# An encoder block in fp32: GELU as one activation, a norm root moved behind the down products, and two more pairs of blocks by seven products

## Chip, cores and metric

The kernel runs on one core of a Trainium2 chip. The metric is the device time of one execution in microseconds. Engines are called by their names in the profile: PE is TensorE (PEld its weight loads), DVE is VectorE, ACT is ScalarE, POOL is GpSimd, SP is SyncE, which here only issues DMAs.

## What is computed

One layer of a bidirectional encoder on 256 tokens and 2048 features, all in fp32. Two attention branches are gated, merged and projected into the residual `x`; then comes the part that matters here, a gated MLP with 5632 hidden features (`D_FF`), and after it a gated embedding term and a last norm.

```python
def rms_norm(x, g):
    y = xf * lax.rsqrt(jnp.mean(xf * xf, axis=-1, keepdims=True) + RMS_EPS)
    return y * g
...
hf = rms_norm(x, ffn_norm[i])
g = dwconv_centred(hf @ w_ffn_gate[i], conv_w[i], conv_b[i])
x = x + (jax.nn.gelu(g) * (hf @ w_ffn_up[i])) @ w_ffn_down[i]
gate_p = jax.nn.sigmoid(rms_norm(x, ple_norm[i]) @ w_ple_gate[i])
x = x + gate_p * (p[i] @ w_ple_proj[i])
return rms_norm(x, final_norm)
```

`jax.nn.gelu` is the form with a tanh by default. The factor `rsqrt(...)` of a norm belongs to a token; it is called the root below.

## The kernel before

**Numbers in two parts.** PE multiplies in a type (`fp32r`) that keeps fewer bits, so each fp32 operand is split in a high and a low part: ScalarE copies it to the high part (L261 for weights, tile `whi`), VectorE subtracts that from the operand for the low part (L262, `wlo`). A product of two operands is three matmuls: high by high, high by low, low by high. Weights come in pieces of sixteen blocks of 128 x 128, by DMAs that SP issues (L238, tiles `raw`), and are split in parts of eight blocks (four at a pair's start). Four buffers each hold `whi` and `wlo`, so splitting runs at most a few parts ahead of PE.

**Jobs.** `_plan` writes the program out as a list of jobs, one after the other on PE. From L102 on:

- `gg`, `g` and `u`: one column block of the gate or up product each, 16 blocks of weights. `product` (L330) issues for each block one matmul with 512 columns (L324) and one with 256 (L325). The hidden features are done in two halves of 22 column blocks; in each half gate and up jobs alternate.
- `d0` and `d1`: the down product of each half, as two jobs (n = 0, 1) of 1024 output columns each.
- `pp` (embedding) and `pg` (its gate): four jobs each; then the output.

When a gate job is done, `after` (L766 to L778) adds its two partial results, multiplies by the root as a row over the tokens (`rt[1]`, L768), applies the convolution's three taps (L770 to L772) and computes the GELU from a square (L774, ScalarE), a product (L775, VectorE), a tanh (L776, ScalarE) and a last product (L777, VectorE). For an up job (L779 to L792) it multiplies by 0.5 and the root (L781) and by the GELU (L789), and splits the result for the down product into `act`; for the first 16 column blocks of a half it also builds sums of two neighbours (`add_up`, L797).

**Seven products in place of eight.** A down job goes over eleven pairs of hidden column blocks. A pair with 2 x 2 quarters (two token halves, two halves of 512 columns) can be done plainly, by eight products, or by seven products of sums of quarters; each product is three matmuls of 512 columns (L400 to L402), so 24 or 21 in all. `_pairs` (L126) gives the order of a job's pairs and which of them go by seven: for the last job, `d1` with n = 1, `[5, 0, 1, 6, 2, 3, 7, 4, 8, 9, 10]` and pairs 0 to 4; for the other three `[8, 0, 1, 2, 3, 9, 4, 5, 6, 7, 10]` and pairs 0 to 7. A pair by seven needs sums of quarters of its weights. They are built long before: POOL's queue fetches the quarters (L286, L287), VectorE subtracts (L299), POOL's queue writes the result to device memory (L303), and SP fetches it back when its pair comes near (L315). `sums_ahead` (in the loop over the jobs) hands this out over the jobs. One more sum is subtracted on the spot (L270), or fetched ready made for pairs 2, 3, 6 and 7 (`WHOLE`); another always on the spot (L272). So a pair by seven costs VectorE and ScalarE four splits (512, 1024, 1024, 1024 columns) and VectorE one or two subtractions of 512 columns.

**Ending a down job.** Four of the seven accumulators (p1, p5, p6, p7) are complete once the last pair by seven is done; then `spread_sums` (L827) runs: a copy of p1 on ScalarE (L830), four sums on VectorE (L835, L840, L841). At the end of the job the other four (p2, p3, p4, c22) follow (from L1085). Where the job is not the last of its columns, each result is written to a row buffer (tile `row`, seven of them, L819) and added to the residual by a DMA on POOL's queue (`to_residual`, L825); the four late ones are copied by ScalarE (L1090). In the last job (`end`) VectorE adds them to the residual in place (L845, and `joined`, L905), but for p1 and the sum with p7, which go by DMA.

**Order around the change.** `at((i, k), f)` puts work ahead of step k of job i; a pair counts two steps. In the last job, step 10 has the squares of the first 1024 columns (`squares_of`, L856, ScalarE), step 18 splits the embedding (`layered`), steps 17, 17, 19, 19 the transposes of features (`flip`: PE L866, ScalarE L454, VectorE L455) for the norm and the products of `pg`. The transposes use the two `pt` banks of PE's accumulator memory, in which p6 and p7 lie in this job. The other features follow in the `pp` jobs. Work marked `keep` holds its order on its engine; other instructions may be put in another order within an engine.

## Time and profile before

| what | us |
|---|---|
| median of 3 runs | 1468.25 |
| lowest and highest run | 1464.38, 1468.91 |
| span of the profiled execution | 1463.2 |
| PE busy | 1449.4 |
| DVE busy | 1137.2 |
| ACT busy | 832.9 |

The profiled execution has no time of its own beside its span, which goes from the first to the last instruction; the runs lie 1.2 to 5.7 us above it. The mean clock that was granted to PE is 0.998. In the profile a row of instructions has: start, duration (both us), engine, line, operation, output and inputs, shape, how often, and in brackets the idle time before it with what ended it. A row of groups has: line, engine, operation, tiles, shape, count, then busy time in us, mean ns of one, and idle time before them in us. A row of the table of windows has the window, its length and for each engine the busy time and the number of instructions.

### The profile page before, as it was taken

The page shows a single profiled execution, that of the slowest core. Times are in us where ns is not written, and L with a number is a line of the kernel's source. Part 1 is how long each engine was busy: PE and PEld are TensorE (multiplying, and loading weights), DVE is VectorE, ACT ScalarE, POOL GpSimd, SP SyncE. Part 2 cuts the span into 40 slices and gives each one's busy share as a digit, 9 for nine tenths or more (in the row PEclk, how much of TensorE's full clock was granted, in tenths as well). Part 3 has the DMA queues.
Part 4 walks back from the last instruction along what each step waited for, and adds up shares of the span by engine and source line. Part 5 has one row for each costly group of instructions (what it writes and reads, how often), then busy time and mean ns, then how long its engine had stood idle before and what let it go on. Part 6 is the DMA issues. An engine that isn't in the chain of part 4 may idle for free.

```text
span 1463.2 us, 20802 instructions
## 1 busy us (share of the span) xinstructions
PE 1449.4 (99%) x7507; PEld 1234.3 (84%) x7507; DVE 1137.2 (78%) x1653; ACT 832.9 (57%) x1196; POOL 107.3 (7%) x178
## 2 busy tenths in 40 slices
PE   9999999999999999999999999999999999999997
PEld 8888888888888888888888888888888888788886
DVE  7687665665665668889998989897999987988665
ACT  7465444444444456665566655675656555666654
POOL 0000000001111100201111100102110100010000
PEclk9999999999999999999999999999999999999999
DMA  9754555557888967978788786989878864797652
GB/s 322 245 177 159 172 170 171 188 178 262 286 314 294 354 229 254 296 237 283 269 293 270 273 284 212 285 287 304 279 273 282 289 244 159 266 294 249 217 193 89
DMA packets 111731, 362.17 MB, mean 248 GB/s; under 512 B 12804, under 2 KB 17924, under 8 KB 111500
## 3 DMA queue, kind: packets, MB, share of 16 engines
q1 hardware_dynamic: 88908, 292.80, 57.5%
q0 software_dynamic: 20560, 63.71, 14.4%
q10 hardware_dynamic: 2160, 4.33, 0.9%
q8 instruction: 59, 0.97, 0.3%
q14 instruction: 44, 0.36, 0.1%
HBM read 324.06 MB, written 27.30 MB: 240 GB/s over the span
## 4 chain that ended last, share of the span: by engine, by line
PE 96%; DVE 1%; issue 1%; DMA 1%; ACT 0%; POOL 0%; POOLq 0%; DVEq 0%; ACTq 0%
PE acc L324 28%; PE acc L325 14%; PE acc L356 9%; PE acc L358 9%; PE acc L357 9%; PE acc L401 7%; PE acc L400 7%; PE acc L402 7%; PE first L324 2%; PE first L325 1%; PE pt L669 1%; DMA raw<-in_wts 0%; PE pt L866 0%; DVE wlo L262 0%; PE sp L628 0%
## 5 line engine op out<-in xcount | busy, mean ns | idle before, releaser
L262 DVE TENSOR_TENSOR wlo<-raw,whi 128x1024 fp32r<-128x1024 f32 (+2 forms) x556 | 650.7, 1181 | 264.3 <-ACT whi L261 258.9
L261 ACT ACTIVATE whi<-raw 128x1024 fp32r<-128x1024 f32 (+2 forms) x556 | 564.2, 1025 | 473.5 <-PE acc L358 188.7
L324 PE MATMUL acc<-mov,whi 128*128 128x512 f32 x1840 | 642.2, 395 | 0.3 <-DVE mov L455 0.3
L325 PE MATMUL acc<-mov,wlo 128*128 128x256 f32 x1840 | 511.0, 278 | 0.0
L324 PEld LDWEIGHTS acc<-mov,whi 128*128 128x128 f32 x1840 | 345.0, 188 | 79.5 <-DVE mov L455 0.6
L325 PEld LDWEIGHTS acc<-mov,wlo 128*128 128x128 f32 x1840 | 346.0, 188 | 0.5
L356 PE MATMUL acc<-whi,mov 128*128 128x512 f32 (+1 forms) x512 | 196.5, 384 | 0.0
L358 PE MATMUL acc<-whi,mov 128*128 128x512 f32 (+1 forms) x512 | 196.3, 383 | 0.0
L357 PE MATMUL acc<-wlo,mov 128*128 128x512 f32 (+1 forms) x512 | 196.2, 383 | 0.0
L356 PEld LDWEIGHTS acc<-whi,mov 128*128 128x128 f32 x512 | 96.7, 189 | 19.3 <-DVE first L444 0.8
L358 PEld LDWEIGHTS acc<-whi,mov 128*128 128x128 f32 x512 | 96.6, 189 | 18.8
L357 PEld LDWEIGHTS acc<-wlo,mov 128*128 128x128 f32 x512 | 96.6, 189 | 18.4
L400 PE MATMUL acc<-whi,act 128*128 128x512 f32 x207 | 80.9, 392 | 0.2 <-ACT whi L261 0.2
L401 PE MATMUL acc<-wlo,act 128*128 128x512 f32 x207 | 80.9, 391 | 0.0
L402 PE MATMUL acc<-whi,act 128*128 128x512 f32 x207 | 80.6, 389 | 0.0
L825 POOL DMA_DIRECT2D x<-row x36 | 31.1, 879 | 380.0 <-ACT row L830 258.1
L262 DVE TENSOR_TENSOR wlo<-sums,whi 128x1024 fp32r<-128x1024 f32 x37 | 45.1, 1219 | 9.9 <-ACT whi L261 9.9
L400 PEld LDWEIGHTS acc<-whi,act 128*128 128x128 f32 x207 | 38.8, 188 | 9.5 <-ACT whi L261 1.5
L401 PEld LDWEIGHTS acc<-wlo,act 128*128 128x128 f32 x207 | 38.9, 188 | 8.9 <-DVE wlo L262 0.9
L401 PE MATMUL acc<-wlo,shl 128*128 128x512 f32 x116 | 45.6, 393 | 0.0
L402 PEld LDWEIGHTS acc<-whi,act 128*128 128x128 f32 x207 | 38.9, 188 | 8.0
L402 PE MATMUL acc<-whi,shl 128*128 128x512 f32 x116 | 45.2, 390 | 0.0
(203 smaller groups left out, 1669.5 us busy)
## 6 DMA issues: line engine op xcount, KB each, us to landing
raw<-in_wts SPq DMA_DIRECT2D x477, 512.0 KB, 5.0
sums<-kept SPq DMA_DIRECT2D x37, 512.0 KB, 5.6
sums<-in_wts POOLq DMA_DIRECT2D x23, 512.0 KB, 6.8
kept<-sums POOLq DMA_DIRECT2D x23, 512.0 KB, 4.1
raw<-in_wts SPq DMA_DIRECT2D x39, 256.0 KB, 4.9
row<-in_wts POOLq DMA_DIRECT2D x37, 256.0 KB, 8.2
x<-row POOLq DMA_DIRECT2D x36, 256.0 KB, 7.7
two<-in_wts POOLq DMA_DIRECT2D x14, 512.0 KB, 8.0
```

Of the source, the lines that this page charges most:

```text
L261: nc.scalar.activation(hi, src, AF.Copy)
L262: ins = nc.vector.tensor_tensor(lo, src, hi.bitcast(F32), op=ALU.subtract)
L324: nc.tensor.matmul(acc, hi[:, o, :], m, start=first, stop=False, skip_group_check=True)
L325: nc.tensor.matmul(acc[:, T:], lo[:, o, :], m[:, :T], start=False, stop=last, skip_group_check=True)
L356: nc.tensor.matmul(acc, xh, hi, start=(k == 0), stop=False)
L357: nc.tensor.matmul(acc, xh, lo, start=False, stop=False)
L358: nc.tensor.matmul(acc, xl, hi, start=False, stop=(k == n - 1))
L400: nc.tensor.matmul(acc, xh, hi, start=(e == 1), stop=False)
L401: nc.tensor.matmul(acc, xh, lo, start=False, stop=False)
L402: nc.tensor.matmul(acc, xl, hi, start=False, stop=(e == uses[name]))
L669: nc.tensor.transpose(p[:, k, t * P:(t + 1) * P], s[:, t, (c + k) * P:(c + k + 1) * P], ident)
L825: keep(nc.gpsimd.dma_start(quarter(n, t, c), a, accum_op=ALU.add))
```

## The change

The GELU becomes one activation with the tanh form. The up products are no longer multiplied by 0.5 and the root; since the root belongs to a token, it is applied to the down products' results instead, each time they are copied, scaled or added: as a scale from memory (`token_scale`) on ScalarE, or in a VectorE instruction that multiplies and adds. For this the first copy of p1 is made twice (unscaled for the sums, scaled for the residual), and finished sums that leave by DMA are scaled in place by ScalarE. The row of the first p1 copy then takes the last sum. In the last job, seven pairs go by seven products instead of five, in another order, and the transposes stand two steps later. The job list and everything ahead of the MLP stay the same.

```diff
-        return [5, 0, 1, 6, 2, 3, 7, 4, 8, 9, 10], range(5)
+        return [7, 0, 1, 2, 8, 3, 4, 5, 6, 9, 10], range(7)
...
-            w = ff.tile([P, T], F32, name="gw", bufs=2)
-            nc.scalar.activation(w, c, AF.Square, scale=math.sqrt(0.044715))
-            nc.vector.scalar_tensor_tensor(w, w, 1.0, c, op0=ALU.add, op1=ALU.mult)
-            nc.scalar.activation(w, w, AF.Tanh, scale=GELU_C)
-            nc.vector.scalar_tensor_tensor(c, w, 1.0, c, op0=ALU.add, op1=ALU.mult)
+            nc.scalar.activation(c, c, AF.Gelu_apprx_tanh)
             held["gelu", n] = c
         elif kind == "u":
             u = gather(acc)
-            nc.vector.scalar_tensor_tensor(u, u, 0.5, rt[1], op0=ALU.mult, op1=ALU.mult)
...
-    def spread_sums(n, bank, end):
-
+    def spread_sums(n, bank, end, scaled):
+
+        def add(t, c, a):
+            if end and c:
+                q = quarter(n, t, 1)
+                if scaled:
+                    nc.vector.scalar_tensor_tensor(q, a, token_scale(t), q, op0=ALU.mult, op1=ALU.add)
+                else:
+                    nc.vector.tensor_tensor(q, q, a, op=ALU.add)
+                return
+            if scaled:
+                nc.scalar.activation(a, a, AF.Copy, scale=token_scale(t))
+            to_residual(n, t, c, a)
+
+        base = row()
+        nc.scalar.activation(base, bank["p1"], AF.Copy)
+        if scaled:
+            first = row()
+            nc.scalar.activation(first, bank["p1"], AF.Copy, scale=token_scale(0))
+            to_residual(n, 0, 0, first)
+        else:
+            add(0, 0, base)
         u = row()
-        nc.scalar.activation(u, bank["p1"], AF.Copy)
-        to_residual(n, 0, 0, u)
...
+        nc.vector.tensor_tensor(u, bank["p6"], base, op=ALU.add)
+        v = row()
+        nc.vector.tensor_tensor(v, bank["p7"], u, op=ALU.add)
+        w = base if scaled else row()
+        nc.vector.tensor_tensor(w, bank["p5"], v, op=ALU.add)
         nc.vector.tensor_tensor(u, bank["p5"], u, op=ALU.add)
...
+        add(1, 0, v)
+        add(0, 1, u)
+        add(1, 1, w)
+
+    def token_scale(t):
+        return held["scale"][:, t:t + 1]
...
-    def joined(n, t, acc, parts):
+    def joined(n, t, acc, parts, scaled):
 
         r = res[:, t, n * W4:(n + 1) * W4]
-        nc.vector.tensor_tensor(r, acc, r, op=ALU.add)
+        if scaled:
+            nc.vector.scalar_tensor_tensor(r, acc, token_scale(t), r, op0=ALU.mult, op1=ALU.add)
+        else:
+            nc.vector.tensor_tensor(r, acc, r, op=ALU.add)
...
+            at((i + 3, 6), lambda: nc.vector.tensor_scalar(held["scale"], rc[1], 1.0, None, op0=ALU.mult))
...
-                                  [(i + 1, k) for k in (17, 17, 19, 19)]):
+                                  [(i + 1, k) for k in (19, 19, 21, 21)]):
...
-                    nc.scalar.activation(a, acc[name], AF.Copy)
+                    nc.scalar.activation(a, acc[name], AF.Copy, scale=1.0 if kind == "o" else token_scale(t))
```

More of the change, by code (lines that the diff above doesn't have):

```diff
@@ L44 @@
 TWINS = [slice(t, T, 2) for t in range(2)]
-GELU_C = math.sqrt(2.0 / math.pi)
 QA, KA, VA = 0, 8, 10
@@ L825, in to_residual @@
         keep(nc.gpsimd.dma_start(quarter(n, t, c), a, accum_op=ALU.add))
-    def spread_sums(n, bank, end):
-        u = row()
-        nc.scalar.activation(u, bank["p1"], AF.Copy)
-        to_residual(n, 0, 0, u)
-        last = u
-        for name in ("p6", "p7"):
-            v = row()
-            nc.vector.tensor_tensor(v, bank[name], last, op=ALU.add)
-            last, u = v, last
-        u, v = u, last
-        to_residual(n, 1, 0, v)
-        w = row()
-        nc.vector.tensor_tensor(u, bank["p5"], u, op=ALU.add)
-        nc.vector.tensor_tensor(w, bank["p5"], v, op=ALU.add)
-        for t, a in enumerate((u, w)):
-            if end:
-                q = quarter(n, t, 1)
-                nc.vector.tensor_tensor(q, q, a, op=ALU.add)
-            else:
-                to_residual(n, t, 1, a)
+    def spread_sums(n, bank, end, scaled):
[18 more added lines that the diff above has]
+            add(0, 0, base)
+        u = row()
+        nc.vector.tensor_tensor(u, bank["p6"], base, op=ALU.add)
[3 more added lines that the diff above has]
+        nc.vector.tensor_tensor(w, bank["p5"], v, op=ALU.add)
+        nc.vector.tensor_tensor(u, bank["p5"], u, op=ALU.add)
+        add(1, 0, v)
[3 more added lines that the diff above has]
+        return held["scale"][:, t:t + 1]
     def layered(pr):
@@ L971, in _encoder @@
                 held[a] = marks[:, e]
-            held["half"] = marks[:, 3, 0, :2]
+            held["half"], held["scale"] = marks[:, 3, 0, :2], marks[:, 4, 0, :2]
             for e in range(3):
@@ L1086, in _encoder @@
                 if end:
-                    joined(2 * n + c, t, acc[name], parts)
+                    joined(2 * n + c, t, acc[name], parts, kind != "o")
                 else:
                     a = row()
-                    nc.scalar.activation(a, acc[name], AF.Copy)
+                    nc.scalar.activation(a, acc[name], AF.Copy, scale=1.0 if kind == "o" else token_scale(t))
                     to_residual(n, t, c, a)
```

2 lines of the change are left out of this document (1 added, 1 removed).

## The prediction

> **What bounds the kernel now.** I read the page first, then the table of windows, then the time line of TensorE, then the other engines where a down job ends.
>
> ```profile
> span 1463.2 us, 20802 instructions
> PE 1449.4 (99%) x7507; PEld 1234.3 (84%) x7507; DVE 1137.2 (78%) x1653; ACT 832.9 (57%) x1196; POOL 107.3 (7%) x178
> PE 96%; DVE 1%; issue 1%; DMA 1%; ACT 0%; POOL 0%; POOLq 0%; DVEq 0%; ACTq 0%
> ```
>
> The third line is the chain that ended last: 96% of it is PE. A busy PE need not be PE at its pace, so the pace itself is read from starts. First a stretch of a gate or up job, then one of a down job (first and last row of each):
>
> ```profile
> 1195.08 0.40 PE L324 MATMUL acc<-mov,whi 128*128 128x512 f32 x1
> ...
> 1204.45 0.39 PE L324 MATMUL acc<-mov,whi 128*128 128x512 f32 x1
> ```
>
> ```profile
> 1332.11 0.39 PE L400 MATMUL acc<-whi,shl 128*128 128x512 f32 x1
> ...
> 1337.55 0.39 PE L400 MATMUL acc<-whi,act 128*128 128x512 f32 x1
> ```
>
> In the first, 27 blocks (a 512-column and a 256-column matmul each) take 9.37 us: 0.347 us each, 0.452 ns a column. In the second, 24 matmuls of 512 columns take 5.44 us: 0.2267 us each, 0.443 ns a column. The reader is to see that both stages issue at nearly the same time per column, though VectorE's load differs. What can be won is matmuls left out, and the few places where the pace breaks. The starts of the down stages, and of what follows them, give the size of these breaks:
>
> ```profile
> 884.32 0.39 PE L400 MATMUL acc<-whi,act 128*128 128x512 f32 x1
> ...
> 994.08 0.39 PE L324 MATMUL acc<-mov,whi 128*128 128x512 f32 x1
> ...
> 1239.46 0.40 PE L400 MATMUL acc<-whi,act 128*128 128x512 f32 x1
> ...
> 1338.24 1.03 PE L866 MATMUL pt<-ident,x 128*128 128x128 f32 x8
> ...
> 1353.67 0.39 PE L356 MATMUL acc<-whi,pw 128*128 128x512 f32 x1
> ```
>
> A pair by seven products is 21 matmuls, one by eight is 24. Both jobs of d0 and the first of d1 have 8 x 21 + 3 x 24 = 240, the last 5 x 21 + 6 x 24 = 249. So d0 should last 480 x 0.2267 = 108.8 us and lasts 109.8: 1.0 lost. d1 should last 489 x 0.2267 = 110.9, with two sets of eight transposes (0.8 each) 112.4, and lasts 114.2: 1.8 lost. Together 2.8 us.
>
> **The change, part by part.** *GELU and the norm root.* These groups go (one activation takes their place):
>
> ```profile
> L781 DVE SCALAR_TENSOR_TENSOR u<-u,rms 128x256 f32<-128x256 f32 x44 | 18.6, 424 | 1.1
> L775 DVE SCALAR_TENSOR_TENSOR gw<-gw,c 128x256 f32<-128x256 f32 x44 | 18.5, 421 | 2.7 <-ACT gw L774 2.7
> L777 DVE SCALAR_TENSOR_TENSOR c<-gw,c 128x256 f32<-128x256 f32 x44 | 18.4, 419 | 2.6 <-ACT gw L776 2.6
> L776 ACT ACTIVATE gw<-gw 128x256 f32<-128x256 f32 x44 | 18.3, 416 | 30.0 <-DVE gw L775 30.0
> L774 ACT ACTIVATE gw<-c 128x256 f32<-128x256 f32 x44 | 18.1, 411 | 8.6 <-DVE c L772 8.1
> ```
>
> VectorE loses 44 x (424 + 421 + 419) ns = 55.6 us. ScalarE loses 827 ns and gains one GELU each time; no row shows it; between nothing and the 827 ns of both I take the 416 of the Tanh, the nearest row: 18.1 us saved. Of this, what reaches the end?
>
> ```profile
> 660.00:890.00 230.00, 230.00 (x1321) 200.87 (x1320) 205.58 (x363) 135.66 (x215) 23.82 (x44) 1.00 0.78 269
> 1294.20:1353.70 59.50, 59.29 (x270) 48.77 (x269) 50.13 (x60) 39.36 (x56) 6.61 (x8) 1.00 0.88 267
> ```
>
> (Columns after the length: PE, PEld, DVE, ACT, POOL, clock, DMA share, GB/s.) In the first row VectorE is busy 205.6 of 230 us, and PE all of it at the pace above; nothing of the 55.6 us is on the path, and I count 0. The one place where it shows is the entry into a down stage, where PE meets the pairs by seven while VectorE still finishes the last up products. There it goes
>
> ```profile
> 890.27 0.68 DVE L272 TENSOR_TENSOR raw<-raw 128x512 f32<-128x512 f32 x1
> ...
> 895.64 0.69 DVE L272 TENSOR_TENSOR raw<-raw 128x512 f32<-128x512 f32 x1
> ```
>
> without idling, 5.37 us for one pair whose quarter sum is not ready made, against 21 x 0.2267 = 4.76 on PE. VectorE now arrives earlier by the two last L781 (0.85 us) and up to two of L775 and L777 (0.85). Of the 2.8 us lost I put half, 1.2, at the two entries and take back 0.9 of it.
>
> [...]
>
> *The activation table.* The program loads one table, at its start:
>
> ```profile
> L210 ACT ACT_TABLE_LOAD  x1: 1283/1283/1283, 1.7 to 1.7; - x1
> ```
>
> If GELU needs another, 1.28 us come on ScalarE at the first gate column, and once more if Tanh has to come back. ScalarE is idle 94 us of the first window; I take 0, and up to 1.3 where it isn't covered. [...] No run here has shown a switch so far.
>
> *The root at the down results.* One small VectorE instruction in the first gate jobs: 0. In the three down jobs whose sums go out by DMA, ScalarE gets a second copy of p1 and three scalings of finished sums, and its four last copies get a scale from memory.
>
> ```profile
> L1090 ACT ACTIVATE row<-acc 128x512 f32<-128x512 f32 x16 | 8.9, 592 | 9.4 <-DMA x<-row 6.2 <-PE acc L324 3.1
> L912 ACT ACTIVATE row<-acc,marks 128x512 f32<-128x512 f32 x8 | 5.5, 684 | 7.9 <-PE acc L358 7.9
> ```
>
> By these a copy costs 592 ns and one with a scale from memory 684: 4 x 0.68 + 4 x 0.09 = 3.1 us more per job. This adds waits on ScalarE for VectorE, with the next weight splits behind them. The end of the first job of d0, ScalarE, VectorE and POOL:
>
> ```profile
> 933.35 0.57 ACT L830 ACTIVATE row<-acc 128x512 f32<-128x512 f32 x1
> 933.83 2.00 ACT L261 ACTIVATE whi<-raw 128x1024 fp32r<-128x1024 f32 x2
> ...
> 941.57 0.60 ACT L1090 ACTIVATE row<-acc 128x512 f32<-128x512 f32 x1 [1.29 <-DMA x<-row]
> 942.07 1.05 ACT L261 ACTIVATE whi<-sums 128x1024 fp32r<-128x1024 f32 x1
> ```
>
> ```profile
> 936.13 1.41 DVE L835 TENSOR_TENSOR row<-acc,row 128x512 f32<-128x512 f32 x2
> ```
>
> ```profile
> 934.36 0.89 POOL L825 DMA_DIRECT2D x<-row  x1 [73.89 <-ACT row L830]
> ...
> 941.77 0.85 POOL L825 DMA_DIRECT2D x<-row  x1 [1.80 <-DMA x<-row]
> ```
>
> Four sums of 0.7 each, from 936.13 on, are ready at 937.5 (the second) to 938.9; ScalarE sits between its splits (to 935.83) and the last copy (941.57) long enough for 3 x 0.68. The last copy waits for the first of these DMAs to free a row buffer; that one now starts a copy (0.6) later. The split at 942.07 with its VectorE part ends near 944.4; PE needs it 27 matmuls into the next job, about 884.3 + 240 x 0.2267 + 0.5 lost = 939.2, and 6.1: 945.3. So 0.6 us later costs nothing there. It costs at the end of d0, where PE already waits for that copy:
>
> ```profile
> 997.99 0.70 PE L490 MATMUL misc<-rdg,ones 128*128 128x256 f32 x2 [0.57 <-ACT row L1090]
> ```
>
> +0.5 there. Both ends for a boundary: 0, and the two cases priced as rivals.
>
> *Seven pairs, not five, in the last job.* PE: 6 matmuls less, 6 x 0.2267 = **-1.36 us**. VectorE: a pair by eight takes two splits,
>
> ```profile
> L262 DVE TENSOR_TENSOR wlo<-raw,whi 128x1024 fp32r<-128x1024 f32 (+2 forms) x556 | 650.7, 1181 | 264.3 <-ACT whi L261 258.9
> ```
>
> 2.4 us; by seven it takes 5.4 (pair 5) or, with one subtraction less since its sum is ready made, 4.7 (pair 6): +5.3, so 55.4 of some 58 us of the last job instead of 50.1 of 59.5. The sums of the two pairs are built during the second half's gate and up jobs (seven more DMAs on POOL's queue, POOL being busy 23.8 of 230 us there; five subtractions of 0.68 on VectorE, which gains 27.8 there): 0. The new order has runs 0-1-2 and 3-4-5-6 with one pair by eight ahead of each; the other jobs have two runs of four and keep the pace but for the entry. New is that the four squares of the first job's columns fall on the start of the run of four:
>
> ```profile
> 1319.77 0.62 ACT L856 ACTIVATE row<-x 128x512 f32<-128x512 f32 x1
> ...
> 1322.23 3.46 ACT L261 ACTIVATE whi<-raw 128x1024 fp32r<-128x1024 f32 x4
> ```
>
> ```profile
> 1324.28 0.73 PE L400 MATMUL acc<-whi,act 128*128 128x512 f32 x2 [0.21 <-ACT whi L261]
> ```
>
> They hold ScalarE for 2.5 us, and PE idles for the split behind them. A pair by eight followed; now three more pairs by seven do, VectorE having 5.4 + 5.4 + 4.7 us of work in 14.3. Between 0 and that 1.2 I take +0.8. The sums then leave one pair (24 matmuls, 5.44 us) closer to the end, the first transposes move with them. Their DMA goes out as
>
> ```profile
> 1338.57 0.85 POOL L825 DMA_DIRECT2D x<-row  x1 [3.82 <-DVE row L835]
> ```
>
> ```profile
> 1353.57 1.88 DVE L905 TENSOR_TENSOR x<-acc,x 128x512 f32<-128x512 f32 x3
> ```
>
> and is needed by the second row's group. From issue to landing:
>
> ```profile
> x<-row POOLq DMA_DIRECT2D x36, 256.0 KB, 7.7
> ```
>
> By this median 7.3 us were spare; less 5.4 and a scaling of 0.7, about 1 is left: 0, or 1 to 2 if late.
>
> **Sum** on the profiled execution: -1.36 - 0.9 + 0.5 + 0.8 = -1.0, span 1462.2. The median of the runs lies 5.05 above the span; I add it: **1467.2 us**. About 0.3% (4.4 us) is what a measurement of this kernel can tell from no change: faster is below 1463.85, slower above 1472.65.
>
> **Rivals.**
> *All breaks go.* -1.36 and all 2.8 of the down stages, and the 0.6 or so of 997.99: -4.8, 1463.4. For it: VectorE is freed just ahead of both stages. Against: the squares and the DMA landings stay. 0.11.
> *VectorE bounds the gate and up jobs.* Then the 55.6 us come back: 1412.6. For it: its 205.6 of 230 us busy. Against: the even 0.347 us. 0.02. [...]
> *The last job becomes VectorE's.* After the sums are due, PE has 48 matmuls and 16 transposes, 12.5 us; VectorE has four splits (4.7), six sums (4.1) and eight parts of features:
>
> ```profile
> L455 DVE SCALAR_TENSOR_TENSOR mov<-pt,cl,mov 128x256 fp32r<-128x256 f32 x32 | 14.0, 478 | 5.6 <-ACT mov L454 5.5
> ```
>
> 3.8 us, in all 12.6. In d0 VectorE reached the sums 2.2 us after PE had made them (936.13 against 884.3 + 216 x 0.2267 + 0.6 lost at the entry = 933.9). Late by that much, PE waits 2.3 us at the transposes: 1469.5. It decides whether VectorE has caught up when the sums are due. 0.16.
> *ScalarE's scalings stand ahead of the splits.* Then ScalarE idles from 934.6 to 937.5 and scales until 939.6, the splits of 933.83 end at 941.6, four copies at 943.8, the sums' split at 944.8 and its VectorE part at 946.0: 0.7 late for 945.3, and the splits behind it more. With 1 to 2 us at three job ends: +3 to +6, 1470.2 to 1473.2. It decides where VectorE reaches the sums later than ScalarE's next split is due. 0.13, half of it slower.
> ***Slower*: the last copy waits for the fourth DMA.** The p1 copy's buffer now carries the last sum. If the eighth row is put there, ScalarE waits not for the DMA of 934.36 (landed by 941.6) but for that of 941.77 (some 949.5): 8 us, less 1 spare, at three ends: +21, 1488. It decides by which buffer is given out; with the second p1 copy's, freed first, nothing happens. 0.08.
>
> **How the numbers follow.** Forecast 0.50. Faster 0.11 + 0.02 = 0.13. Slower 0.08 + 0.07, and 0.03 of the VectorE case: 0.18. Within: 0.69. The range 1463.3 to 1472.0 holds the forecast, the first and third rival and half the fourth.
>
> **What would show it.** Right: six matmuls fewer, the gate stage still at 0.347, d1 near 113, VectorE some 47 us less. Wrong: an L1090 wait over 5 us (fourth DMA), whi released by L835's successors (scalings ahead), transposes L866 with idle before them in the last job, or a table load followed by an idle PE. The prediction is wrong altogether if the gate and up jobs change their pace.

## The result, and the profile after

The changed kernel takes 1479.82 us (median of 6 runs, 1478.39 to 1483.16), the kernel before beside it 1467.57 (6 runs, 1464.38 to 1471.74): ratio **1.0082**, 95% interval 1.0067 to 1.0098. It is 0.8% slower, where 1467.2 and no measurable difference had been forecast. The span grew from 1463.2 to 1476.8 us, by 13.6. One run of e3 (the one that was profiled), one of e13 and one of the kernel before ran at a granted clock of 0.56 to 0.75 and took 1799 us or more; no number below contains them.

From the page of the kernel after: the head, the busy times, the chain that ended last.

```profile
span 1476.8 us, 20712 instructions
PE 1455.8 (99%) x7501; PEld 1235.5 (84%) x7501; DVE 1104.2 (75%) x1534; ACT 827.3 (56%) x1171; POOL 110.9 (8%) x185
...
PE 76%; issue 13%; DMA 5%; DVE 3%; ACT 2%; POOL 0%; ACTq 0%; POOLq 0%; DVEq 0%
```

The six matmuls are gone (7507 to 7501), VectorE is busy 33 us less, and yet the time rose. In the chain, DMA has grown from 1% to 5% and VectorE from 1% to 3%, which points at waits for transfers and for VectorE. (13% of the chain is "issue", time for which the profile shows no wait; that says nothing of TensorE, which is busy 99% as before.) Where the time goes, the starts of the stages on TensorE's time line tell (kernel after; the same places as in the prediction, without the transposes of the last job):

```profile
885.97 0.39 PE L399 MATMUL acc<-whi,act 128*128 128x512 f32 x1
...
996.93 0.39 PE L323 MATMUL acc<-mov,whi 128*128 128x512 f32 x1
...
1245.71 0.39 PE L399 MATMUL acc<-whi,act 128*128 128x512 f32 x1
...
1363.02 0.39 PE L355 MATMUL acc<-whi,pw 128*128 128x512 f32 x1
```

The rows are the first matmuls of d0, of the second half, of d1 and of the first `pp` job. Taking for each stage the time from its first matmul to the next stage's first, the 13.6 us are:

| stage | before, us | after minus before |
|---|---|---|
| up to the out products | 551.6 | -0.2 |
| out products | 85.0 | +1.7 |
| first half's gate and up jobs | 247.7 | +0.1 |
| d0 | 109.8 | +1.2 |
| second half's gate and up jobs | 245.4 | +3.4 |
| d1 | 114.2 | +3.1 |
| tail (`pp`, `pg`, output) | 109.5 | +4.2 |

The pace of the gate and up jobs is unchanged in this profile; all of the loss stands at a few places. Three of them follow.

**The entry of the second half.** TensorE, then ScalarE and POOL ahead of it, kernel after:

```profile
999.98 0.28 PE L324 MATMUL acc<-mov,wlo 128*128 128x256 f32 x1
1002.77 1.22 PE L489 MATMUL misc<-rdg,ones 128*128 128x256 f32 x2 [2.51 <-ACT row L1102]
1003.44 0.99 PE L323 MATMUL acc<-mov,whi 128*128 128x512 f32 x1
...
1004.43 0.63 PE L323 MATMUL acc<-mov,whi 128*128 128x512 f32 x1
```

```profile
990.60 0.58 ACT L836 ACTIVATE row<-acc 128x512 f32<-128x512 f32 x1
991.08 1.04 ACT L260 ACTIVATE whi<-raw 128x1024 fp32r<-128x1024 f32 x1
992.02 0.68 ACT L839 ACTIVATE row<-acc,marks 128x512 f32<-128x512 f32 x1
...
1002.03 0.69 ACT L1102 ACTIVATE row<-acc,marks 128x512 f32<-128x512 f32 x1 [2.95 <-DMA x<-row]
```

```profile
993.10 0.85 POOL L819 DMA_DIRECT2D x<-row  x1 [37.79 <-ACT row L839]
```

POOL in the kernel before, the same DMA:

```profile
988.74 0.85 POOL L825 DMA_DIRECT2D x<-row  x1 [35.14 <-ACT row L830]
```

The wait is the one of the row at 997.99 in the prediction: 0.57 us before, 2.51 now. Read backwards: the last late copy (1002.03) waited for the row buffer whose DMA left at 993.10. It left so late because the *scaled* copy of p1 (L839), the one that is sent, comes after the plain one (L836) and after a weight split that the build put between the two. Against the start of d0 the DMA left 2.7 us later than before (993.10 - 885.97 = 107.1; before 988.74 - 884.32 = 104.4). And behind the idle time a matmul of 512 columns takes 0.63 us instead of 0.40, with a granted clock of 0.50 in the table of windows (the column after POOL):

```profile
1001.00:1002.00 1.00, 0.00 (x0) 0.00 (x0) 0.00 (x0) 0.00 (x0) 0.00 (x0) 1.00 1.08 352
1002.00:1003.00 1.00, 0.23 (x1) 0.23 (x2) 0.00 (x0) 0.96 (x2) 0.76 (x1) 0.75 1.07 301
1003.00:1004.00 1.00, 1.00 (x3) 0.82 (x4) 0.30 (x1) 1.00 (x2) 0.08 (x1) 0.50 1.08 307
1004.00:1005.00 1.00, 1.00 (x4) 0.81 (x4) 1.00 (x2) 0.89 (x2) 0.00 (x0) 0.50 1.12 238
1005.00:1006.00 1.00, 1.00 (x5) 0.90 (x4) 1.00 (x1) 0.00 (x0) 0.56 (x1) 0.54 1.11 203
```

0.25 + 0.5 + 0.5 + 0.46 = 1.7 us of clock are lost, nearly all of it while matmuls run. 1.9 us more idle time and some 1.5 of half clock are the 3.4 of this stage.

**The entry of the first `pg` job.** VectorE, then TensorE, kernel after:

```profile
1373.36 0.87 DVE L454 SCALAR_TENSOR_TENSOR mov<-pt,cl,mov 128x256 fp32r<-128x256 f32 x2
1376.27 1.23 DVE L1038 TENSOR_SCALAR end<-end 128x2048 f32<-128x2048 f32 x1 [2.03 <-DMA end<-in_last_gain]
1377.41 0.87 DVE L454 SCALAR_TENSOR_TENSOR mov<-pt,cl,mov 128x256 fp32r<-128x256 f32 x2
```

```profile
1375.60 0.39 PE L357 MATMUL acc<-whi,pw 128*128 128x512 f32 x1
1378.04 0.76 PE L355 MATMUL acc<-whi,mov 128*128 128x512 f32 x1 [2.05 <-DVE mov L454]
1378.60 0.63 PE L356 MATMUL acc<-wlo,mov 128*128 128x512 f32 x1
```

The last features, which TensorE needs at once, stand behind the scaling of the last norm's gain, which is first used by L927 at 1404.20 and waits for its transfer. Neither line is touched by the change. In the kernel before, the build had put the same scaling (L1026) behind the features and it waited for nothing to speak of:

```profile
1364.16 0.88 DVE L455 SCALAR_TENSOR_TENSOR mov<-pt,cl,mov 128x256 fp32r<-128x256 f32 x2 [0.70 <-ACT mov L454]
1365.21 1.23 DVE L1026 TENSOR_SCALAR end<-end 128x2048 f32<-128x2048 f32 x1 [0.17 <-DMA end<-in_last_gain]
```

2.05 us of idle time and another 1.7 of half clock.

**The end of the out products**, which the change leaves alone but for the order in which sums are handed out. ScalarE before, ScalarE after, TensorE before and after:

```profile
626.80 0.63 ACT L856 ACTIVATE row<-x 128x512 f32<-128x512 f32 x1 [2.94 <-DMA x<-row]
...
627.43 0.82 ACT L454 ACTIVATE mov<-pt,cl 128x256 fp32r<-128x256 f32 x2
628.14 1.06 ACT L261 ACTIVATE whi<-raw 128x1024 fp32r<-128x1024 f32 x1
```

```profile
627.17 0.63 ACT L864 ACTIVATE row<-x 128x512 f32<-128x512 f32 x1 [5.25 <-DMA x<-row]
...
627.80 1.04 ACT L260 ACTIVATE whi<-raw 128x1024 fp32r<-128x1024 f32 x1
628.75 0.45 ACT L453 ACTIVATE mov<-pt,cl 128x256 fp32r<-128x256 f32 x1
```

```profile
630.18 1.09 PE L866 MATMUL pt<-ident,x 128*128 128x128 f32 x8 [0.19 <-PE acc L402]
```

```profile
631.62 1.21 PE L874 MATMUL pt<-ident,x 128*128 128x128 f32 x8 [1.28 <-issue]
```

The square at 627.17 waits for its transfer, and the first features stand behind it; after, a split has also slipped in between. The transposes come 1.28 us late (0.19 before). The profile names no releaser for them ("issue"); that they wait for the accumulator bank which the features free is a reading, which e13 to e15 test. How much of the 1.7 us is the change's is not shown: in the kernel before and the six that leave this stage's code alone (e1, e2, e7, e9, e10, e11) it takes from 0.0 to +3.2 us, one profile each.

### The profile page after: what moved, and what is told of

Read it like the earlier page. It is cut to its first block, busy times and chain, and to the rows that moved or that the text cites. A ratio compares the mean times of both kernels' runs of the same rounds, so it can differ in the third digit from the quotient of the medians.

```text
span 1476.8 us, 20712 instructions
## 1 busy us (share of the span) xinstructions
PE 1455.8 (99%) x7501; PEld 1235.5 (84%) x7501; DVE 1104.2 (75%) x1534; ACT 827.3 (56%) x1171; POOL 110.9 (8%) x185
## 4 chain that ended last, share of the span: by engine, by line
PE 76%; issue 13%; DMA 5%; DVE 3%; ACT 2%; POOL 0%; ACTq 0%; POOLq 0%; DVEq 0%
PE acc L323 26%; PE acc L324 13%; PE acc L355 9%; PE acc L357 9%; PE acc L356 9%; DMA x<-row 3%; DVE wlo L261 2%; PE acc L400 2%; PE acc L401 2%; PE first L323 2%; PE acc L399 1%; ACT whi L260 1%; DMA raw<-in_wts 1%; PE first L324 1%; DMA sums<-in_wts 1%
## 5 line engine op out<-in xcount | busy, mean ns | idle before, releaser
L400 PE MATMUL acc<-wlo,act 128*128 128x512 f32 x197 | 77.2, 392 | 0.8 <-DVE wlo L261 0.8
L399 PE MATMUL acc<-whi,act 128*128 128x512 f32 x197 | 77.4, 393 | 0.5 <-ACT whi L260 0.5
L401 PE MATMUL acc<-whi,act 128*128 128x512 f32 x197 | 77.0, 391 | 0.0
L400 PE MATMUL acc<-wlo,shl 128*128 128x512 f32 x124 | 50.1, 404 | 1.0 <-DVE wlo L261 0.4
L401 PE MATMUL acc<-whi,shl 128*128 128x512 f32 x124 | 48.4, 390 | 0.0
L399 PE MATMUL acc<-whi,shl 128*128 128x512 f32 x124 | 47.9, 390 | 0.0
L260 ACT ACTIVATE whi<-sums 128x1024 fp32r<-128x1024 f32 x39 | 41.0, 1051 | 9.5 <-PE acc L323 4.1
L441 DVE TENSOR_TENSOR u<-acc,t 128x256 f32<-128x256 f32 x100 | 41.8, 418 | 6.1 <-ACT t L437 6.1
```

The lines of the kernel that those rows point to most:

```text
L260: nc.scalar.activation(hi, src, AF.Copy)
L399: nc.tensor.matmul(acc, xh, hi, start=(e == 1), stop=False)
L400: nc.tensor.matmul(acc, xh, lo, start=False, stop=False)
L401: nc.tensor.matmul(acc, xl, hi, start=False, stop=(e == uses[name]))
L441: nc.vector.tensor_tensor(u, acc[:, :T], t, op=ALU.add)
```

## The experiments

Two theories were tried. **Q**: the cost is one of queues. On ScalarE or VectorE an instruction that waits for a transfer to land, or a block of instructions that nobody needs yet, stands ahead of the splits or features that TensorE needs next, and the root at the down results (and the new order that the build makes of the program) puts it there. **V**: VectorE is too full in the down jobs, above all with two more pairs by seven. All kernels below compute the whole result. Each ratio is against runs of the kernel before taken beside it; a stage's difference is one profile against the one profile of before. Seven of the sixteen profiles read here have the second half's gate and up jobs at a second, slower pace, 4.7 us in all, also in kernels without the change; it is told of in the last section and is marked * where a stage time holds it.

**e1: GELU alone** in the kernel before.

```diff
-            w = ff.tile([P, T], F32, name="gw", bufs=2)
-            nc.scalar.activation(w, c, AF.Square, scale=math.sqrt(0.044715))
...
-            nc.vector.scalar_tensor_tensor(c, w, 1.0, c, op0=ALU.add, op1=ALU.mult)
+            nc.scalar.activation(c, c, AF.Gelu_apprx_tanh)
...
-            nc.vector.scalar_tensor_tensor(u, u, 0.5, rt[1], op0=ALU.mult, op1=ALU.mult)
+            nc.vector.tensor_tensor(u, u, rt[1], op=ALU.mult)
```

> Only the GELU becomes one activation; the up product keeps its root (the factor 0.5 goes, VectorE still multiplies). Theory Q (the loss comes from ScalarE and VectorE queues in which an instruction that waits for a DMA to land stands ahead of weight splits, and the root at the down results puts it there) expects the time before within 2 us, one table load more, no PE idling over 1 us at the start of the second half's gate jobs or of the gate of the embedding. Theory V (VectorE is too full in the down jobs because of the two more pairs) expects the same here. A rival, that the activation itself or its table costs something, expects a few us more in the gate and up jobs.

Measured: 1467.69 us, ratio 1.0002 (0.9987 to 1.0018). All stages are within 0.2 us of before. VectorE is busy 1111.8 us, 25 less, and that is worth nothing; the second table load (shown below for the kernel after) costs nothing that shows. Both theories expected this.

**e2: seven pairs alone** in the kernel before.

```diff
-        return [5, 0, 1, 6, 2, 3, 7, 4, 8, 9, 10], range(5)
+        return [7, 0, 1, 2, 8, 3, 4, 5, 6, 9, 10], range(7)
...
-                                  [(i + 1, k) for k in (17, 17, 19, 19)]):
+                                  [(i + 1, k) for k in (19, 19, 21, 21)]):
```

> Only the last job's seven pairs and the later transposes; GELU and root as before. Theory Q expects within 2 us of the time before (PE has 6 matmuls, 1.4 us, less). Theory V expects +5 to +8 us, in the last down job (+2 to +3) and at the start of the embedding's gate jobs (+4), since VectorE has as much to do there as in the changed kernel.

Measured: 1470.47 us, ratio 1.0025 (1.0011 to 1.0038). Out products +3.2, second half +4.6*, d1 -0.4, tail +1.7. The six matmuls bring 0.4 of their 1.36 us in d1 and lose it in the tail, in which TensorE idles 0.88 us for the last features. The median is 3.6 us above that of the kernel before, which neither theory had; the +3.2 in the out products is in a stage that this edit leaves alone.

**e3 and e8: GELU and the root, five pairs**: the changed kernel with the diff of e2 undone.

> The changed kernel without the pairs: the last job has five pairs by seven in the old order and the old transposes. Theory Q expects +6 to +9 us over before: the start of the second half's gate jobs +3.4, the first down stage +1.2, the output projection +1.7, the start of the last job +1.3. Theory V expects +2 at most, and no idling over 1 us at those places.

> GELU as one function and the norm root at the down results, with five pairs in the last down job as before: the same kernel that stood at 1.0047 of before, run for a profile of its stages. Theory Q: the entry of the second half of the feed-forward stage costs about 3 us (idle time behind the late copies, and half clock), the boundary within each down job about 1.3, and the last down job and the tail lose little, since VectorE there has no more than before. Theory V: nothing is lost at the entry of the second half (VectorE has no sum of pairs more there than before), so the loss would have to stand in the down jobs themselves.

Measured: e3 1475.08 us, ratio 1.0047 (1.0027 to 1.0067), e8 1477.24, ratio 1.0069 (1.0048 to 1.0089). The root carries most of the loss, as Q had it. Stages of e8: out products +1.6, d0 +1.1, second half +10.0*, d1 +1.0, tail 0.0. The entry of the second half, TensorE:

```profile
1003.98 1.22 PE L489 MATMUL misc<-rdg,ones 128*128 128x256 f32 x2 [3.23 <-ACT row L1102]
```

Less the 4.7 of the second pace that entry costs 5.3 us. V has no loss at this place. The tail is as before: there the root alone costs nothing.

**e4: scaled copy first.** The changed kernel with the copy that is sent ahead of the one that is kept:

```diff
-        base = row()
-        nc.scalar.activation(base, bank["p1"], AF.Copy)
         if scaled:
             first = row()
             nc.scalar.activation(first, bank["p1"], AF.Copy, scale=token_scale(0))
             to_residual(n, 0, 0, first)
-        else:
+        base = row()
+        nc.scalar.activation(base, bank["p1"], AF.Copy)
+        if not scaled:
             add(0, 0, base)
```

> The changed kernel, with the scaled copy of p1 written ahead of the plain one, so that its DMA starts earlier. Theory Q expects that the last copy at the end of the first down stage waits some 1.5 to 2.5 us less, and that PE loses 2 to 4 us less there than the changed kernel: 3 us of the 13.6 back. Theory V expects no difference of more than 1 us.

Measured: 1474.91 us, ratio 1.0050 (1.0032 to 1.0068). The second half comes back from +3.4 to +0.1, with no half clock; d0 from +1.2 to +0.4, d1 from +3.1 to +1.8. TensorE at the entry:

```profile
1000.48 0.70 PE L489 MATMUL misc<-rdg,ones 128*128 128x256 f32 x2 [0.67 <-ACT row L1102]
```

The order of two copies is worth some 0.3%, as Q had it. Here the `pg` entry got worse (2.95 us of idle time, tail +5.2): the gain's transfer landed later and the features stood behind its scaling.

**e5: no scaling of the gain.** The changed kernel, the factor moved into squares that are there anyway:

```diff
-            nc.vector.tensor_scalar(held["lg"], held["lg"], math.sqrt(D), None, op0=ALU.mult)
...
-        keep(nc.scalar.activation(row(), r, AF.Square, accum_out=parts[:, t, n:n + 1]))
+        unit = D ** -0.5 if parts is held["ss3"] else 1.0
+        keep(nc.scalar.activation(row(), r, AF.Square, scale=unit, accum_out=parts[:, t, n:n + 1]))
...
-        nc.vector.tensor_scalar(e, e, D * EPS, None, op0=ALU.add)
+        nc.vector.tensor_scalar(e, e, EPS, None, op0=ALU.add)
```

> The changed kernel whole, but VectorE's scaling of the last norm's gain by sqrt(D) (128x2048, 1.23 us, it waited 2.03 us for its transfer ahead of the last two features) is gone: the squares of the last norm are scaled by 1/D instead, inside an instruction that is there anyway. Theory Q (what costs is an instruction that waits for a transfer ahead of splits or features on the same engine): the last features start about 1375.2 instead of 1377.41, the idle time of TensorE at the entry of the first ple gate job falls from 2.05 us to some 0.3, and with it goes the half clock after it (some 1.7 us), so the tail comes back by about 3.8 us and the kernel stands at about 1.0056 of before. Theory V (VectorE is simply too full in the last down job): only the 1.23 us of the row itself come back at most, the features stay late behind the joined sums, and the kernel stands at about 1.0075 of before.

Measured: 1476.28 us, ratio 1.0065 (1.0043 to 1.0087). The tail comes back from +4.2 to +1.3: 2.9 us, more than twice the 1.23 of the row itself, less than the 3.8 of theory Q. Of the rest, 0.64 us is idle time at the same place, which is not the gain's.

**e6: both**, the diffs of e4 and e5 in the changed kernel.

> Both orders mended in the changed kernel: the scaled copy of the first product's sums goes ahead of the plain one, as in the run that stood at 1.005 of before, and the scaling of the last norm's gain is gone. Theory Q: the two costs are separate places and add, so the tail (there 2.95 us of idle time and the half clock behind it, 4.6 us together) comes back, and the kernel stands at about 1.002 of before, 1470 us. Theory V: d1 and the tail stay about as they are in that run (+1.8 and +5 us over before), and the kernel stands at 1.004 to 1.005.

Measured: 1474.93 us, ratio 1.0048 (1.0033 to 1.0063): by the ratio theory Q missed, and V's 1.004 to 1.005 came out; but the tail, which V left at +5, came back. The profiled run took 1471.5, its span is +6.3: out products +1.6, second half +0.6, d1 +1.6, tail +1.3. The two mends do add in their stages (second half and tail), but the out products, d1 and the rest of the tail were not on the list. In d1, ScalarE and TensorE:

```profile
1323.83 0.62 ACT L865 ACTIVATE row<-x 128x512 f32<-128x512 f32 x1
...
1326.29 1.56 ACT L260 ACTIVATE whi<-raw 128x1024 fp32r<-128x1024 f32 x2
```

```profile
1328.64 0.50 PE L400 MATMUL acc<-wlo,act 128*128 128x512 f32 x1 [0.76 <-DVE wlo L261]
```

The four squares of the first columns stand in one block ahead of a split.

**e7: GELU and seven pairs, no scaling of the gain**: the diffs of e1, e2 and e5 in the kernel before.

> The kernel before with GELU as one function and seven pairs, without the norm root at the down results, and without the scaling of the last norm's gain. With the pairs alone the tail was 1.7 us longer, of which 0.88 us was idle time at the entry of the first ple gate job behind that scaling. Theory Q: that idle time goes, the six matmuls (1.36 us) are won, and the kernel stands at 0.999 of before. Theory V: the two further pairs overload VectorE in the last down job whatever stands in its queue, and the kernel stays at 1.002 as with the pairs alone.

Measured: 1471.75 us, ratio 1.0023 (1.0006 to 1.0040). d1 +0.1, tail +1.5, TensorE at the `pg` entry 0.66 us idle with nothing in front of the features. Q missed, V is right here.

**e9, e10, e11: five, six, seven pairs** with GELU, no root, no scaling of the gain, and the squares spread over four steps. The diffs of e1 and e5 in the kernel before, with that of e2 for seven, and in all three:

```diff
-                        at((i + 1, 10), squares_of, c, t, parts)
+                        at((i + 1, (10, 12, 14, 16)[2 * t + c] if kind == "d1" else 10), squares_of, c, t, parts)
```

Six pairs: `[6, 0, 1, 2, 7, 3, 4, 5, 8, 9, 10], range(6)`, transposes at the steps for five.

> First of a series of one size: GELU as one function, no norm root at the down results, no scaling of the last norm's gain, and the four squares in the last down job at four steps instead of one (they stand as 3.2 us in one block ahead of a split on ScalarE); five pairs as in the kernel before. Theory Q and theory V expect the same here: 1.000 of before, at most 0.3 us off it in the last down job, tail equal to before. It is the point against which the next two are read.

> As the run with five, with six pairs by seven products. Three matmuls (0.68 us) go from the last down job and one more sum of pairs (some 2.4 us of VectorE) comes. Theory Q: nothing queues badly now, so 0.68 us are won and the tail stays. Theory V: VectorE carries the excess into the entry of the first ple gate job, so the last down job is 0.7 shorter and the tail 0.7 longer, nothing is won.

> As the run with five, with seven pairs as in the change. Without the spread squares the last down job came out 0.1 us longer than before and the tail 1.5 longer, though six matmuls (1.36 us) are gone. Theory Q: the squares in one block cost the last down job some 0.7 us of it, so this job comes out 0.6 us shorter than before; the tail's 1.5 stays if it is VectorE's. Theory V: VectorE's excess costs more than the six matmuls give: last down job and tail together 1 to 1.5 us longer than with five pairs, and the kernel stands at 1.001 of it.

| pairs | us | ratio (interval) | d1 | tail |
|---|---|---|---|---|
| 5 | 1465.40 | 0.9993 (0.9978 to 1.0009) | -0.6 | 0.0 |
| 6 | 1466.95 | 0.9991 (0.9978 to 1.0004) | +0.1 | -0.1 |
| 7 | 1467.01 | 0.9991 (0.9975 to 1.0008) | +0.1 | +1.6 |

The medians say nothing between these three; the stages do. From five to seven pairs, d1 and tail together get 2.3 us longer, though 1.36 us of matmuls go: the two pairs cost 3.7 us. With seven, TensorE waits 0.9 us at the transposes in d1 and 0.68 at the `pg` entry, there for features of VectorE. The rest is many delays of at most 0.25 us and 0.3 us behind the last matmul, and no run shows what causes these. VectorE near the end of d1, with seven pairs and with five:

```profile
1356.50 2.47 DVE L902 TENSOR_TENSOR x<-acc,x 128x512 f32<-128x512 f32 x4
```

```profile
1355.90 0.69 DVE L902 TENSOR_TENSOR x<-acc,x 128x512 f32<-128x512 f32 x1 [1.03 <-PE acc L402]
```

With seven (first row) the four joins wait for nothing: VectorE comes late. With five (e9) it is there first and waits 1.03 us for TensorE's accumulator. With six, d1 is already 0.7 us longer than with five, though 0.68 us of matmuls go, and the tail only breaks with the seventh; Q had the 0.7 won and V had it lost in the tail. What V had for seven, 1 to 1.5 us lost, is nearest. The count is not the only difference: the order of the pairs changes with it, and with seven the transposes stand two steps later.

**e12: the whole change, mended** by the diffs of e4, e5 and e9, and with the order of the sums behind the out products as in the kernel before:

```diff
         nc.vector.tensor_tensor(v, bank["p7"], u, op=ALU.add)
+        if not scaled:
+            add(1, 0, v)
...
-        add(1, 0, v)
+        if scaled:
+            add(1, 0, v)
```

> The whole change with all orders mended: the scaled copy ahead of the plain one, no scaling of the last norm's gain, the squares at four steps, and in the out products (whose results are not scaled) the transfer of the fourth sum handed out right behind the second sum, as before. Theory Q: the out products come back to within 0.2 us of before (they are 1.6 us longer in five of the five runs with the new order of sums, but also 3.2 in one with the old order), the last down job comes to +0.6, the entry of the second half stays at +0.5 and the tail at +1.3: 1.002 of before. Theory V: the out products do not depend on the order and stay at +1.6, the last down job stays at +1.6, and the kernel stays at 1.0045.

Measured: 1472.05 us, ratio 1.0030 (1.0012 to 1.0048). d1 comes back to -0.1, from +1.6 in e6 (and +3.1 in the changed kernel): the block of squares had been what e6 left there. The ratio lies between the two theories. But the out products came out at +2.9: the order of the sums is not what makes them longer, and that cause fell.

**e13, e14, e15: the squares behind the out products two steps later**, after the first features:

```diff
-                        at((i + 1, (10, 12, 14, 16)[2 * t + c] if kind == "d1" else 10), squares_of, c, t, parts)
+                        at((i + 1, (10, 12, 14, 16)[2 * t + c] if kind == "d1" else 12), squares_of, c, t, parts)
```

e13 is the root with five pairs, e14 five pairs without the root, e15 the whole change (with its own order of the sums in the out products), all with the other mends.

> GELU as one function and the norm root at the down results, with five pairs in the last down job, and all orders mended: scaled copy ahead of the plain one, no scaling of the last norm's gain, squares of the last down job at four steps, and the squares behind the out products two steps later, behind the first four features. Theory Q: the root costs only where it stands ahead of something, so the out products come to within 0.4 us of before, the first down stage and the entry of the second half to +0.5 each, the last down job and the tail to +0: 1.001 of before at the same pace of the second half. Theory V: VectorE has the root's scalings in the down jobs whatever the order, and the kernel stays at 1.003.

> The same without the root: GELU as one function, five pairs, no scaling of the last norm's gain, squares spread in the last down job, and behind the out products two steps later. Theory Q: as the run with five pairs before, 0.6 us won in the last down job, and the 0.3 us of idle time at the end of the out products gone as well, also where the transfer lands late: 0.999 of before. If the squares were not what holds the transposes there, the out products stay at 85.0 us or come out longer.

> The whole change with all orders mended, squares behind the out products two steps later (the order of the sums there as the change has it). Theory Q: the out products come back from +2.9 us, as in the mended whole change without this, to +0.2 or below, the other stages as there: first down stage +0.7, last down job 0, tail +1.3, 1.0015 of before at the same pace. If the loss is in the later landing itself, the out products stay at +1 to +3.

| kernel | us | ratio (interval) | out products | d0 | second half | d1 | tail |
|---|---|---|---|---|---|---|---|
| e13, root, 5 pairs | 1466.04 | 0.9994 (0.9982 to 1.0007) | +0.1 | +0.7 | +4.7* | -0.8 | 0.0 |
| e14, no root, 5 pairs | 1464.41 | 0.9982 (0.9968 to 0.9996) | -0.7 | +0.3 | +0.5 | -0.6 | 0.0 |
| e15, root, 7 pairs | 1469.04 | 1.0019 (1.0001 to 1.0036) | -0.5 | 0.0 | +5.1* | +0.2 | +1.3 |

ScalarE and TensorE at the end of the out products in e14:

```profile
626.54 0.87 ACT L454 ACTIVATE mov<-pt,cl 128x256 fp32r<-128x256 f32 x2 [1.16 <-DVE mov L455]
627.30 0.63 ACT L853 ACTIVATE row<-x 128x512 f32<-128x512 f32 x1
```

```profile
629.75 1.03 PE L863 MATMUL pt<-ident,x 128*128 128x128 f32 x8
```

The features go first, the squares no longer wait, the transposes have no idle time before them. All three kernels come out at +0.1 or below in the out products (one profile each), where the thirteen profiles with the squares two steps earlier lie at 0.0 to +3.2; e15 differs from e6 in this stage by nothing else (-0.5 against +1.6). So the excess is the features behind a square that waits for a transfer, as Q had it. With five pairs and mended orders the root costs nothing that shows against the kernel before (1.0069 to 0.9994), and it wins nothing: e14, the same without it, has a median 1.6 us lower, with intervals that overlap. What remains of the whole change is what seven pairs cost in the tail and d1. The lowest median is e14's: GELU as one function, five pairs, no root, mended orders. It is 0.18% below the kernel before, and its interval does not reach 1; but it is the best of fourteen kernels, and its interval overlaps that of e9 (0.9993), which differs only by the two steps.

## Why the prediction was wrong

The forecast of no measurable change failed: the sum of its terms was -1.0, the span grew by 13.6. Step by step:

- **"The median of the runs lies 5.05 above the span; I add it": not an offset.** Each run lies 1.7 to 2.1 us above its own span; the rest of the 5.05 is that the profiled execution of before was one of the shorter ones. It matters little beside 13.6.
- **GELU and the table: right.** The GELU costs 407 ns (416 taken), and the table load ahead of the first one costs nothing that shows. With all three VectorE lines gone, the first half's gate and up jobs take 247.8 us (247.7 before), so the rival by which VectorE bounds them is out. In e1 VectorE's busy time fell by 25 us and the time by none (ratio 1.0002). The "some 47 us less" for VectorE came out at 33: the durations of all its rows fell by 45.5 us, but rows overlap (before, one of 0.42 us starts at 1103.20 and the next at 1103.54), so a sum of durations overstates the busy time that goes.

The load in the groups of the kernel after (busy us, mean ns, idle time before):

```profile
L772 ACT ACT_TABLE_LOAD x1 | 1.3, 1283 | 0.0
```

- **"-0.9" at the entries of the down stages: wrong, 0.** In e1, where L775 and L777 are gone, d0 and d1 take 109.8 and 114.2 us as before; where L781 is gone too and the orders are mended, d0 takes +0.7 (e13) and 0.0 (e15). VectorE's earlier arrival wins nothing at those entries. (Half of the 2.8 us is 1.4, not 1.2; that changes nothing here.)
- **"+0.5 there" at the end of d0: right place, wrong size, and the step that failed first.** It was 3.4 (5.3 in e8 by the same count). "That one now starts a copy (0.6) later" took the scaled copy to follow the plain one directly. The build put a split between the two and d0 itself ran 1.2 us late, so the DMA left 2.7 us later relative to d0's start; and the 2.51 us of idle time were followed by half clock (0.50 for 3.41 us), which no row of before could show. e4 undoes it.
- **"So 0.6 us later costs nothing there" at the job boundary of d0: nearly.** d0 lost 1.2; with the scaled copy first 0.4 (e4), in the mended kernels 0.0 to 0.7.
- **"+0.8" for the squares in the last job: too small.** The mechanism was named, but d1 lost 3.1 us in place of winning 0.5; spread squares (e12) bring back all of the 1.6 that e6 had left.
- **"-1.36" for six matmuls: they are gone, their time is not.** Seven pairs cost 3.7 us against five, 2.3 after the 1.36 won (e9 to e11). The third rival (VectorE late in the last job, chance 0.16) named the engine; that its figure is 2.3 too is luck, for the rival's was a wait at the transposes alone, with the 1.36 won counted beside it. Those waits are 0.9 us in e11, and 0.68 stand at the `pg` entry, where the prediction did not look.
- **"0, or 1 to 2 if late" in the tail: wrong.** The tail lost 4.2. 2.9 of them come back in e5 without touching the sum's DMA: they were the gain's scaling ahead of the last features, an instruction in no part of the diff, and the half clock behind it. The other 1.3 us are as large as in the kernels with seven pairs and no root (1.5 to 1.7 in e2, e7 and e11).
- **The out products were not in the prediction at all.** They took 1.7 us more, of which an unknown part is the change's.
- **The last two rivals did not come.** In the kernel after ScalarE's scalings ran behind the next splits, and no late copy of a down job waited over 2.95 us.

The common fault: the working took the order of instructions on ScalarE and VectorE as it stood in the profile of before and inserted the new ones into it. The order is made anew in each build for all that is not marked `keep`, and three of the losses are in lines that the change doesn't touch.

## What to carry to other kernels

When TensorE is at its pace, ask at each stage's entry what stands *ahead* of the one instruction that it waits for, and take out of that queue what waits for a transfer or is needed later: the copy that is sent goes ahead of the one that is kept, and long blocks for later use are spread. The edit that saved 25 us of busy time on VectorE alone gave nothing by itself (e1, ratio 1.0002), and a saving on TensorE that is paid for with work of an engine near its limit is first measured as a series of one size (e9 to e11). After any edit compare the whole order of each engine, not only the edited lines.

## What the runs showed of the hardware

**Half clock after short idle time.** Idle times of TensorE of 2.05 and 2.51 us (after), 2.95 (e4) and 3.23 (e8) were followed by half clock (a matmul of 512 columns took 0.63 us in each); one of 1.95 (e12) and one of 2.19 us (e5) were not (0.39 to 0.40 soon after), nor the 1.66 of e8. The length of the idle time alone did not decide. A trace records when the granted clock changes. In the kernel after it goes from 1.00 to 0.50 at 1002.50 and back at 1005.91, the same at 1377.97 and 1381.38: 3.41 us each time, the two beginnings 375.47 us apart, which is 110 steps of 3.413. Windows cut at these steps, in the kernel after around both places, then in e5 around its 2.19 us:

```profile
999.09:1002.50 3.41, 1.17 (x7) 0.75 (x6) 0.00 (x0) 0.47 (x1) 0.62 (x2) 1.00 1.07 318
1002.50:1005.91 3.41, 3.13 (x9) 2.67 (x10) 2.21 (x2) 2.39 (x4) 1.05 (x2) 0.50 1.10 260
```

```profile
1374.56:1377.97 3.41, 1.42 (x7) 0.84 (x5) 1.70 (x3) 3.41 (x7) 0.00 (x0) 1.00 0.52 187
1377.97:1381.38 3.41, 3.35 (x8) 2.70 (x9) 3.41 (x4) 0.54 (x1) 0.00 (x0) 0.50 0.21 66
```

```profile
998.39:1001.80 3.41, 2.74 (x16) 2.13 (x14) 0.73 (x1) 1.55 (x3) 1.76 (x2) 1.00 1.06 329
1001.80:1005.22 3.42, 1.90 (x10) 1.67 (x11) 0.97 (x1) 2.64 (x4) 0.85 (x1) 1.00 1.09 319
```

TensorE is idle for 2.24 and 1.99 us of the windows ahead of half clock. Counted in such steps from the first change on record (5.81), no other window of the kernel after ahead of the one with its last matmul has more than 1.18 us without a matmul (630.45 to 633.86), and none is followed by half clock. In the kernel before, counted from 5.47, none has more than 0.62 (643.76 to 647.17), and the clock falls to 0.50 only at 1456.13, behind the last matmul (1453.21). The 2.19 us of e5 are cut by a window's end: 0.67 us in one, 1.52 in the next. Each of these two half clocks lasted one window, at a loss of 1.7 us of clock; the mean clock of that profiled run is 0.995, as is that of e8's. About the same idle time thus cost 1.7 us more in one kernel (2.05 us, after) and nothing in another (2.19, e5). That it depends on where the idle time falls is a reading of these few windows. The six runs of the kernel after have mean granted clocks of 0.995 (the profiled one) to 0.998, the latter as in the kernel before, so its two half-clock windows are not in every run.

**A second pace of the gate and up jobs.** Of the same 200 us, in the kernel before and in e8:

```profile
1020.00:1220.00 200.00, 200.00 (x1156) 174.90 (x1155) 180.78 (x317) 119.47 (x188) 17.88 (x33) 1.00 0.78 270
```

```profile
1020.00:1220.00 200.00, 200.00 (x1134) 173.50 (x1133) 161.53 (x260) 109.17 (x168) 17.89 (x33) 1.00 0.79 266
```

22 matmuls fewer, at a granted clock of 1.00, with no idle time and spread evenly: 200 / 578 = 0.346 us a block against 200 / 567 = 0.353, some 4.7 us over the second half. It holds from the entry of the half to its end, never in the first half. It is not the change's: e9 (no root, five pairs) has it, the kernel after has not, and the runs of the kernel before fall into two groups (beside e13 to e15: 19 of 1464.7 to 1467.4 us, 10 of 1469.2 to 1471.6). It was seen in 7 of 16 profiles. What sets it stays open, and it widens every interval given here.
